# A two-block transformer on one core: the third weight's parts kept in the query tiles, the first norm's sum taken sooner, the last norm scaled in wider pieces

## The chip, the cores and the metric

The kernel runs on one core of one Trainium2 chip. The metric is the device time of one execution in microseconds (us), the median of several runs. All shapes are fixed: 512 tokens of width 1024, all data in fp32.

## What is computed

Two blocks, one after the other. The first mixes tokens with four kinds of heads and adds a gated feed-forward part; the second is a short convolution, a feed-forward part, latent attention, a feed-forward part and a last norm. Cut to what the change touches:

```python
def first_block(x, ...):
    mixed = token_mix(rms_norm(x, norm1_g), w_in, ...)   # one product with w_in, then four kinds of heads
    x = x + mixed @ w_out
    return x + conv_glu_ffn(rms_norm(x, norm2_g), ...)

def second_block(x, ...):
    ...                                                  # short convolution, FFN, latent attention
    h = h + swiglu_ffn(rms_norm_2(h, mla_ffn_norm_g), w13, w2)
    return rms_norm_2(h, final_norm_g)                   # the last norm

def rms_norm(x, g):
    return x * rsqrt(mean(x * x, axis=-1) + EPS) * g
```

## The kernel before, in words

Everything lies transposed: 128 features on the partitions, 512 tokens along a row, so that x is 8 tiles of 128x512. A product of fp32 precision is made from two parts of each operand, a rounded one (h) and what is left (l): three matmuls (h by h, h by l, l by h) for each of 8 steps, 24 for one output tile. `split` (L111) makes a weight's parts: ScalarE copies h (L113), VectorE subtracts (L118). A weight comes by one DMA into one of 3 `raw` buffers, and its parts go into one of 2 `wh` and 2 `wl` buffers, which come free when the product that used them ends.

A norm is put off: the matmuls take x times its gain, and the row factor r (1/rms) is multiplied in when VectorE takes the product out of PSUM. r comes from the sum of squares `acc` (`squares`, L157, each square on ScalarE, each add on VectorE), a matmul with a tile of ones (`mean`, L1543), and Ln, Exp and one Newton step (`rsqrt_wide`, L137).

The first phase, `mix`, is planned by hand. `conduct` (L768) writes TensorE's queue in order: it keeps a count `clk` of TensorE time, steps the products of `w_in` (in the order `ORDER`: sm0, gq0, gk0, then by availability gv0, lq0, lf0, lv0), and between the steps puts the pieces of three lanes of strands, each due at a time that the strand itself gives (`yield`). The first lane holds `mean`, `small` (gates from tile sm0), `gdn0`, `gdn1`; the second the linear attention (`hg0`, `gla`, `hg1`); the third `fox0`, `fox1`. The orders on the other engines come from the tile framework: a priority by place in the program, and readiness by its own cost model; each engine then runs its list in order.

Around the change: `start` (L1511) loads x and the first two weights in pieces and makes their parts; `conduct` steps the two products together (48 matmuls, L782 to L786), then starts the third and the fourth, whose PSUM has tag `fps`; `mean` is due `Y_MEAN` after its strand starts, which is at the end of the first two. Until `mean` is done nothing can be taken out of PSUM; then sm0 is scaled by r (`scaled`, L915), which gives back the first `mm` buffer of PSUM, then gq0 (`convolved`, L949, into a tile z of which there is one in this phase, and a convolution of three VectorE operations, L237). `first_low` (L152 to L154) makes the next weight's subtraction on VectorE stand behind the last operation of r. `small` transposes sm0, makes the gate logarithms on ScalarE, and `Y_SM` later multiplies them (`gg`, L980) with a triangle on TensorE. `hg_bounds` (L1245) are a dozen small operations on ScalarE and VectorE in turn.

`final` (L332) is the last product with the last norm: the last of 8 tiles is made in two halves of 256 tokens, and `write` (L365) multiplies each half's 8 tiles with r, 6 on VectorE and 2 on GpSimd, into `raw` tiles, and stores them two tiles at a time, all from SyncE's queue.

Of the kernel before, what the change touches and what calls it, by code (L numbers as in the profile page):

```python
# [9 lines left out]
F32 = mybir.dt.float32  # L10
F32R = mybir.dt.float32r
# [3 lines left out]
ACTF = mybir.ActivationFunctionType  # L15
ALU = mybir.AluOpType
AX = mybir.AxisListType

S = 512
D = 1024  # L20
KD = D // 128
# [3 lines left out]
CHUNK = 8  # L25


class Builder:
# [108 lines left out]
    def rsqrt_wide(self, ps, scale, tag, n=S, short=False):  # L137


        nc = self.nc  # L140
        r = self.t(tag="u", bufs=3)[:, :n]
        nc.scalar.activation(out=r, in_=ps, func=ACTF.Ln, scale=scale, bias=self.epsD)
        v = self.t(tag="s", bufs=3)[:, :n]
        nc.scalar.activation(out=r, in_=r, func=ACTF.Exp, scale=-0.5)
        if n < S or short:
            nc.vector.tensor_scalar(out=v, in0=ps, scalar1=scale, scalar2=EPS, op0=ALU.mult, op1=ALU.add)
        else:
            nc.scalar.activation(out=v, in_=ps, func=ACTF.Identity, scale=scale, bias=self.epsD)
        nc.vector.tensor_tensor(out=v, in0=v, in1=r, op=ALU.mult)
        nc.vector.scalar_tensor_tensor(out=v, in0=v, scalar=-0.5, in1=r, op0=ALU.mult, op1=ALU.mult)  # L150
        out = self.t(tag=tag, bufs=3 if tag == "u" else 1) if tag else v
        i = nc.vector.scalar_tensor_tensor(out=out, in0=v, scalar=1.5, in1=r, op0=ALU.add, op1=ALU.mult)  # L152
        if short:
            self.first_low = i.ins  # L154
        return out

    def squares(self, xs, adder):  # L157
# [174 lines left out]
    def final(self, w, xs, gi, out):  # L332


        nc = self.nc
        last = KD - 1
        g = [self.gains[:, gi * KD + k : gi * KD + k + 1] for k in range(KD)]
        acc = self.b("acc")
        for c in range(last):
            ps = self.dense(w, c, xs)  # L340
            nc.vector.tensor_tensor(out=self.x[c], in0=self.x[c], in1=ps, op=ALU.add)
            sq = acc if c == 0 else self.t(tag="sq")
            nc.scalar.activation(out=sq, in_=self.x[c], func=ACTF.Square)
            if c:
                nc.gpsimd.tensor_tensor(out=acc, in0=acc, in1=sq, op=ALU.add)
            nc.scalar.activation(out=self.x[c], in_=self.x[c], func=ACTF.Copy, scale=g[c])
        ws = self.weight(w, last, len(xs))
        n = S // 2
        for half in range(2):
            ts = slice(half * n, half * n + n)  # L350
            ps = self.product(ws, xs, ts)
            x = self.x[last][:, ts]
            nc.vector.tensor_tensor(out=x, in0=x, in1=ps, op=ALU.add)
            sq = self.t(tag="sq")[:, :n]
            nc.scalar.activation(out=sq, in_=x, func=ACTF.Square)
            nc.scalar.activation(out=x, in_=x, func=ACTF.Copy, scale=g[last])
            if half:
                self.write(out, 0, r)
            sp = self.pst()[:, :n]
            nc.tensor.matmul(out=sp, lhsT=self.ones, rhs=acc[:, ts], start=True, stop=False)  # L360
            nc.tensor.matmul(out=sp, lhsT=self.ones, rhs=sq, start=False, stop=True)
            r = self.rsqrt_wide(sp, 1.0 / D, None, n)
        self.write(out, 1, r)

    def write(self, out, half, r):  # L365

        nc = self.nc
        n = S // 2
        ts = slice(half * n, half * n + n)
        for i in range(2):  # L370
            y = self.raw.tile([128, CHUNK * 128], F32, tag="raw", name="raw").rearrange("p (k t) -> p k t", t=n)
            for k in range(4):
                eng = nc.gpsimd if k == 1 else nc.vector
                eng.tensor_tensor(out=y[:, k], in0=self.x[4 * i + k][:, ts], in1=r, op=ALU.mult)
                if k % 2:
                    ks = slice(4 * i + k - 1, 4 * i + k + 1)
                    nc.sync.dma_start(out=out[ks, :, ts].rearrange("k p t -> p k t"), in_=y[:, k - 1 : k + 1])


NH = 8  # L380
# [12 lines left out]
class Mla(Builder):  # L393
# [244 lines left out]
TILES = {  # L638
    n: i
    for i, n in enumerate(  # L640
        "sm0 gq0 gq1 gk0 gk1 gv0 gv1 lq2 lk2 lv2 lv3 lq0 lq1 lf0 lf1 lv0 lv1 rq0 rq1 rk0 rk1 fv0 fv1 "
        "gz0 gz1 lz0 lz1 lz2 lz3".split()
    )
}
T_SMALL, T_GQ = TILES["sm0"], TILES["gq0"]
ORDER = (
    "sm0 gq0 gk0 lf1 gq1* lq2 gv0* lq0* lf0 lk2 lv0 lq1* rq0 lv3 gk1* lv2 "
    "rk1 fv0 gv1 lv1 rk0 gz0* rq1 lz0* fv1 gz1 lz3* lz2 lz1*"
)
# [9 lines left out]


Y_FIN, Y_FOX, Y_GDN, Y_SM = 8.3, 8.64, 4.0, 5.33
Y_MEAN = 12.3
C_MEAN = 4.0
C_SILU = 4.8
Y_ROW = 2.66
DUE = 4.78
# [7 lines left out]
class Mix(Mla):  # L674
# [93 lines left out]
    def conduct(self, jobs, lanes):  # L768
# [8 lines left out]
        last = []  # L777
        self.last = last
        xs = [(k, *x) for k, x in enumerate(self.xs)]
        nxt, dense, held = None, [], []  # L780

        two = [(self.stepped(ws, xs, "mm"), jobs.pop(0)) for ws in self.firsts]  # L782
        for i in (0, 0, 1, 1, *(0, 1) * (KD - 2)):
            ps, k = next(two[i][0])
            if k == KD - 1:
                held.append((ps, *two[i][1][2:]))  # L786
        outs, parked, row = list(range(KD)), [], None
        while True:

            for i, lane in enumerate(lanes):  # L790
                if strands[i] is None and lane and all(n in ready for n in lane[0][0]):
                    need, name, gen, rings = lane.pop(0)
# [4 lines left out]
            while held and "mean" in self.over:  # L797
                ps, name, post = held.pop(0)
                t = post(ps)
                if t is not None:  # L800
                    ready[name] = max(self.clk, ready["mean"] + C_MEAN) + t
            if nxt is None:
                job = next((j for j in jobs if j[1] in self.over), None)
                if job:
                    jobs.remove(job)
                    nxt = job, self.weight(self.a["w_in"], job[0], KD)
                elif not jobs and outs:
                    c = outs.pop(0)
                    nxt = (c, None, None, self.out_post(c)), self.weight(self.a["w_out"], c, KD)
# [100 lines left out]
    def scaled(self, dst, after=None, last=None):  # L910


        def post(ps):
            y = self.b(dst[0], bufs=2 if dst[0] in ("lv", "fv") else 1)
            self.nc.vector.tensor_tensor(out=y, in0=ps, in1=self.r, op=ALU.mult)  # L915
            if last is not None:
                return self.silus(y, dst, last)
            self.inp[dst] = y
            return LV + (after(y) if after else 0.0)

        return post
# [589 lines left out]
    def start(self, gi):  # L1511


        idle = self.psm.tile([128, S], F32, tag="lps", name="lps", bufs=2)
        for _ in range(11):
            self.nc.tensor.matmul(out=idle[:, :128], lhsT=self.ones, rhs=self.ones, start=True, stop=True)
        nc = self.nc
        self.x = [self.rt("x") for _ in range(KD)]
        cts = T_SMALL, TILES[ORDER.split()[1][:3]]
        raw = [self.raw.tile([128, CHUNK * 128], F32, tag="raw", name="raw") for _ in cts]  # L1520
        h = [self.wh.tile([128, CHUNK * 128], F32R, tag="wh", name="wh") for _ in cts]
        l = [self.wl.tile([128, CHUNK * 128], F32R, tag="wl", name="wl") for _ in cts]
        steps = (("w", 0, 0), ("x", 0), ("x", 1), ("w", 1, 0), ("x", 2), ("x", 3), ("w", 0, 1), ("x", 4),
                 ("w", 1, 1), ("x", 5), ("x", 6), ("x", 7))
        half = lambda i: slice(i * 512, i * 512 + 512)
        for what, i, *part in steps:
            if what == "x":
                nc.sync.dma_start(out=self.x[i], in_=self.a["xT"][i])
            else:
                cs = half(part[0])  # L1530
                nc.sync.dma_start(out=raw[i][:, cs], in_=self.a["w_in"][cts[i], :, cs])
        self.xs = []
        for what, i, *part in steps:
            if what == "x":
                self.xs.append(self.gained(self.x[i], self.gain(gi, i), "x"))
            else:
                cs = half(part[0])
                self.split(raw[i][:, cs], h[i][:, cs], l[i][:, cs])
        col = lambda t, k: t[:, k * 128 : (k + 1) * 128]
        self.firsts = [[(col(h[i], k), col(l[i], k)) for k in range(KD)] for i in range(2)]  # L1540
        self.acc = self.squares(self.x, nc.vector)

    def mean(self):  # L1543
# [57 lines left out]
@with_exitstack  # L1601
def kernel(ctx, tc, aps, out):
    b = Mix(ctx, tc, aps)
    with b.phase("mix", 2, s=4, sq=3, z=1):
        b.start(0)
        b.mla_consts()
        b.mix_consts()
        b.mix()
    b.rope_pool = ctx.enter_context(tc.tile_pool(name="rope", bufs=1))
    with b.phase("ffn"):  # L1610
        b.consts()
        b.conv_glu(2)
        b.conv_mixer(3)
        b.swiglu(5, aps["w13_a"], aps["w2_a"], b.rope_tables())
    with b.phase("mla", 4, "pt"):
        b.mla(4, 6)
    with b.phase("ffn2"):
        b.swiglu(None, aps["w13_b"], aps["w2_b"], out=(7, out))


# [108 lines left out]
```

## Time and profile before

| | |
|---|---|
| median of 3 runs | 1879.36 us (1879.07 to 1899.09) |
| the profiled execution's own time | 1877.87 us |
| its span | 1876.1 us |
| mean granted clock of TensorE | 0.99 |
| TensorE busy | 97% of the span |
| VectorE busy | 56% |
| ScalarE busy | 39% |
| GpSimd busy | 10% |
| chain that ended last | TensorE 87%, VectorE 6%, ScalarE 4% |

Times in the trace are us from the span's start. A row of the timeline gives an instruction's start, its duration, engine, line, operation, what it writes and reads, and in brackets how long its engine had stood idle and what released it. The ends of matmuls are modelled, so the distance from one start to the next tells more than a duration. The granted clock is 1.00 at 2.4 GHz and 0.50 at 1.2 GHz.

### The profile page before, as it was taken

Reading aid. Unit: us, or ns where it says so; the run is one execution under the profiler, and the core shown is the slowest. Engines: PE = TensorE matmul, PEld = TensorE weight load, DVE = VectorE, ACT = ScalarE, POOL = GpSimd, SP = SyncE. Lnnn points to the kernel's source line nnn. Section 1 sums busy time; section 2 is a strip of 40 time slices with the busy share of each in tenths; the row PEclk is TensorE's granted clock in tenths of the full one; section 3 lists DMA queues with packets and bytes.
Section 4 is the critical chain, followed back from the end, with each engine's and each line's share of the span. In section 5 each row is a group of like instructions: output and inputs, shape, how many; then the busy total and the mean of one; then the engine's idle time right before and its main releaser. Section 6 shows DMA issues by size and latency. Waiting matters only on the chain.

```text
span 1876.1 us, 22127 instructions
## 1 busy us (share of the span) xinstructions
PE 1824.9 (97%) x8631; PEld 1509.4 (80%) x8631; DVE 1055.9 (56%) x1624; ACT 740.0 (39%) x1138; POOL 194.2 (10%) x230
## 2 busy tenths in 40 slices
PE   7899989899999999999999999999999999999997
PEld 5788778778888888888888888888777888888886
DVE  5885886767777733455464444333876454444323
ACT  4644455345444432322343232322667432332322
POOL 2320311220000001111110000000011200000001
PEclk8999999999999999999999999999999999999999
DMA  4111111132222333322222222333222222222332
GB/s 165 46 46 46 57 34 35 62 100 99 101 92 100 98 93 93 99 99 92 101 96 101 96 95 101 93 93 97 80 61 74 78 91 100 92 101 92 99 93 76
DMA packets 53368, 162.62 MB, mean 87 GB/s; under 512 B 6544, under 2 KB 13200, under 8 KB 53264
## 3 DMA queue, kind: packets, MB, share of 16 engines
q1 hardware_dynamic: 53136, 161.21, 26.0%
q8 instruction: 67, 1.10, 0.2%
q14 instruction: 37, 0.30, 0.1%
q10 hardware_dynamic: 128, 0.01, 0.0%
HBM read 157.78 MB, written 2.10 MB: 85 GB/s over the span
## 4 chain that ended last, share of the span: by engine, by line
PE 87%; DVE 6%; ACT 4%; issue 1%; POOL 1%; DMA 0%; SPq 0%; DVEq 0%; ACTq 0%; POOLq 0%
PE mm L131 24%; PE mm L133 24%; PE mm L132 24%; PE mm L715 9%; PE gps L715 2%; PE lps L715 2%; PE fps L715 1%; ACT wh L113 1%; DVE lat L1382 1%; DVE wl L118 1%; POOL s L1320 0%; PE ps L586 0%; PE ps L174 0%; DVE ptl L118 0%; DVE nm L589 0%
## 5 line engine op out<-in xcount | busy, mean ns | idle before, releaser
L113 ACT ACTIVATE wh<-raw 128x1024 fp32r<-128x1024 f32 (+3 forms) x309 | 308.7, 1001 | 763.0 <-PE mm L132 463.5
L131 PE MATMUL mm<-xh,wh 128*128 128x512 f32 x1336 | 522.5, 391 | 0.2 <-ACT xh L182 0.2
L132 PE MATMUL mm<-xl,wh 128*128 128x512 f32 x1336 | 521.3, 390 | 0.5 <-DVE xl L183 0.5
L133 PE MATMUL mm<-xh,wl 128*128 128x512 f32 x1336 | 520.6, 390 | 0.0
L118 DVE TENSOR_TENSOR wl<-raw,wh 128x1024 fp32r<-128x1024 f32 (+4 forms) x301 | 366.2, 1217 | 231.2 <-ACT wh L113 228.3
L132 PEld LDWEIGHTS mm<-xl,wh 128*128 128x128 f32 x1336 | 251.0, 188 | 53.8 <-issue 1.2
L131 PEld LDWEIGHTS mm<-xh,wh 128*128 128x128 f32 x1336 | 251.0, 188 | 53.4 <-issue 1.0
L133 PEld LDWEIGHTS mm<-xh,wl 128*128 128x128 f32 x1336 | 251.0, 188 | 52.1 <-issue 0.2
L131 PE MATMUL mm<-hidh,wh 128*128 128x512 f32 (+1 forms) x614 | 237.0, 386 | 0.0
L133 PE MATMUL mm<-hidh,wl 128*128 128x512 f32 (+1 forms) x614 | 235.5, 384 | 0.0
L132 PE MATMUL mm<-hidl,wh 128*128 128x512 f32 (+1 forms) x614 | 234.1, 381 | 0.0
L715 PE MATMUL mm<-xh,wh 128*128 128x512 f32 x292 | 130.7, 448 | 11.6 <-DVE sm L915 5.6
L133 PEld LDWEIGHTS mm<-hidh,wl 128*128 128x128 f32 x614 | 115.5, 188 | 24.3
L132 PEld LDWEIGHTS mm<-hidl,wh 128*128 128x128 f32 x614 | 115.5, 188 | 23.3
L131 PEld LDWEIGHTS mm<-hidh,wh 128*128 128x128 f32 x614 | 115.8, 189 | 21.7 <-ACT wh L113 0.2
L715 PE MATMUL mm<-xl,wh 128*128 128x512 f32 x292 | 118.0, 404 | 0.9 <-DVE xl L183 0.5
L715 PE MATMUL mm<-xh,wl 128*128 128x512 f32 x292 | 117.9, 404 | 0.2 <-DVE wl L118 0.2
L287 DVE TENSOR_TENSOR u<-mm,rb 128x512 f32<-128x512 f32 x44 | 30.4, 691 | 141.2 <-PE mm L133 141.2
L167 POOL TENSOR_TENSOR z<-z,sq 128x512 f32<-128x512 f32 x31 | 51.8, 1672 | 556.7 <-ACT sq L165 519.0
L283 DVE TENSOR_TENSOR u<-mm,rb 128x512 f32<-128x512 f32 x44 | 30.4, 692 | 90.9 <-PE mm L133 90.8
L715 PEld LDWEIGHTS mm<-xh,wh 128*128 128x128 f32 x292 | 57.4, 197 | 25.0 <-issue 8.5
L113 ACT ACTIVATE hidh<-s 128x512 fp32r<-128x512 f32 x66 | 41.7, 632 | 88.3 <-DVE s L264 57.2
(436 smaller groups left out, 2089.6 us busy)
## 6 DMA issues: line engine op xcount, KB each, us to landing
raw<-in_w_a_dram SPq DMA_DIRECT2D x52, 512.0 KB, 3.3
raw<-in_w_b_dram SPq DMA_DIRECT2D x52, 512.0 KB, 3.2
raw<-in_w_up_dram SPq DMA_DIRECT2D x44, 512.0 KB, 3.2
raw<-in_w_in_dram SPq DMA_DIRECT2D x27, 512.0 KB, 3.2
raw<-in_conv_w_in_dram SPq DMA_DIRECT2D x24, 512.0 KB, 3.2
raw<-in_w_down_dram SPq DMA_DIRECT2D x16, 448.0 KB, 3.3
raw<-in_w_a_dram SPq DMA_DIRECT2D x16, 448.0 KB, 3.3
raw<-in_w_b_dram SPq DMA_DIRECT2D x16, 448.0 KB, 3.2
```

The lines of the kernel that those rows point to most:

```text
L113: nc.scalar.activation(out=h, in_=src, func=ACTF.Copy)
L118: (eng or nc.vector).tensor_tensor(out=l, in0=src, in1=h.bitcast(F32), op=ALU.subtract)
L131: nc.tensor.matmul(out=ps, lhsT=h, rhs=xh, start=(k == 0), stop=False)
L132: nc.tensor.matmul(out=ps, lhsT=h, rhs=xl, start=False, stop=False)
L133: nc.tensor.matmul(out=ps, lhsT=l, rhs=xh, start=False, stop=(k == kt - 1))
L167: eng.tensor_tensor(out=acc, in0=acc, in1=sq, op=ALU.add)
L283: nc.vector.tensor_tensor(out=g, in0=ps, in1=r, op=ALU.mult)
L287: nc.vector.tensor_tensor(out=g, in0=ps, in1=r, op=ALU.mult)
L715: self.nc.tensor.matmul(out=out, lhsT=lhsT, rhs=rhs, start=start, stop=stop)
L1382: nc.vector.copy_predicated(out=at.rearrange("p c (n j) -> p c n j", j=2 * b)[:, :, :, b:], mask=self.lmask[:, lv - 1].rearrange("p (n j) ...
```

## The change

Three things. The third weight (gk0) is loaded in `start` and its parts go into the two tiles `lbd0` and `lbd1`, which the linear attention uses for its query tiles later, so that it needs no `wh` and `wl` buffer; its DMA stands in SyncE's queue behind the last tile of x and ahead of the constants. `Y_MEAN` goes from 12.3 to 2.6 and `C_MEAN`, the planner's count from the sum to the first tile, from 4.0 to 3.6; `first_low` is now the scaling of sm0, so the next weight's subtraction stands behind that. In `final` the tiles times gain go to a tile of their own, `xg`; `write` multiplies four tiles with one VectorE operation in place (at the end two and two), none on GpSimd, with fewer stores, the last two from ScalarE's queue. In the last phase there is one z buffer, not two.

```diff
@@ rsqrt_wide
-        i = nc.vector.scalar_tensor_tensor(out=out, in0=v, scalar=1.5, in1=r, op0=ALU.add, op1=ALU.mult)
-        if short:
-            self.first_low = i.ins
+        nc.vector.scalar_tensor_tensor(out=out, in0=v, scalar=1.5, in1=r, op0=ALU.add, op1=ALU.mult)
@@ final
+        self.scaled_x = self.b("xg", shape=(128, KD * S)).rearrange("p (k t) -> p k t", t=S)
-            nc.scalar.activation(out=self.x[c], in_=self.x[c], func=ACTF.Copy, scale=g[c])
+            nc.scalar.activation(out=self.scaled_x[:, c], in_=self.x[c], func=ACTF.Copy, scale=g[c])
-            nc.scalar.activation(out=x, in_=x, func=ACTF.Copy, scale=g[last])
+            nc.scalar.activation(out=self.scaled_x[:, last, ts], in_=x, func=ACTF.Copy, scale=g[last])
@@ write
-        for i in range(2):
-            y = self.raw.tile([128, CHUNK * 128], F32, tag="raw", name="raw").rearrange("p (k t) -> p k t", t=n)
-            for k in range(4):
-                eng = nc.gpsimd if k == 1 else nc.vector
-                eng.tensor_tensor(out=y[:, k], in0=self.x[4 * i + k][:, ts], in1=r, op=ALU.mult)
-                if k % 2:
-                    ks = slice(4 * i + k - 1, 4 * i + k + 1)
-                    nc.sync.dma_start(out=out[ks, :, ts].rearrange("k p t -> p k t"), in_=y[:, k - 1 : k + 1])
+        k0 = 0
+        for many in (4, 4) if half == 0 else (4, 2, 2):
+            ks = slice(k0, k0 + many)
+            y = self.scaled_x[:, ks, ts]
+            nc.vector.tensor_tensor(
+                out=y, in0=y, in1=r[:, :n].unsqueeze(1).to_broadcast([128, many, n]), op=ALU.mult
+            )
+            eng = nc.scalar if half and k0 == 4 else nc.sync
+            eng.dma_start(out=out[ks, :, ts].rearrange("k p t -> p k t"), in_=y)
+            k0 += many
@@
-Y_MEAN = 12.3
-C_MEAN = 4.0
+Y_MEAN = 2.6
+C_MEAN = 3.6
@@ conduct
-        nxt, dense, held = None, [], []
+        dense, held = [], []
...
+        nxt = jobs.pop(0), self.third_ws
@@ scaled
-            self.nc.vector.tensor_tensor(out=y, in0=ps, in1=self.r, op=ALU.mult)
+            i = self.nc.vector.tensor_tensor(out=y, in0=ps, in1=self.r, op=ALU.mult)
+            if dst[0] == "sm":
+                self.first_low = i.ins
@@ start
+        r3 = self.raw.tile([128, CHUNK * 128], F32, tag="raw", name="raw")
+        nc.sync.dma_start(out=r3, in_=self.a["w_in"][TILES[ORDER.split()[2][:3]]])
+        h3, l3 = (self.b(f"lbd{i}", F32R, shape=(128, 1024)) for i in range(2))
+        self.split(r3, h3, l3)
+        self.third_ws = [(col(h3, k), col(l3, k)) for k in range(KD)]
         self.acc = self.squares(self.x, nc.vector)
@@ tile_two_blocks_kernel
-    with b.phase("ffn2"):
+    with b.phase("ffn2", z=1):
```

## Rows read from the trace of the kernel before

**Rows 1.** Profile page, part 1: busy us, share of the span, instructions.

```profile
PE 1824.9 (97%) x8631; PEld 1509.4 (80%) x8631; DVE 1055.9 (56%) x1624; ACT 740.0 (39%) x1138; POOL 194.2 (10%) x230
```

**Rows 2.** TensorE's waits, 0 to 450 us: total us, times, longest us.

```profile
PE fps L715 <- ACT fpt L1496: 6.4, 2, 4.0
PE mm L715 <- DVE sm L915: 5.6, 1, 5.6
PE gps L715 <- DVE gg L980: 5.5, 1, 5.5
```

**Rows 3.** Stretches of 5 us: length, TensorE busy, granted clock, DMA share, GB/s.

```profile
20.00:25.00 5.00, 3.48 (x8) 0.66 0.29 92
...
40.00:45.00 5.00, 4.14 (x10) 0.50 0.30 105
...
60.00:65.00 5.00, 4.21 (x16) 0.50 0.00 0
```

**Rows 4.** Timeline of TensorE, 17 to 66 us.

```profile
17.75 0.39 PE L715 MATMUL mm<-xh,wl 128*128 128x512 f32 x1
21.33 0.64 PE L715 MATMUL mm<-xh,wh 128*128 128x512 f32 x1 [3.19 <-ACT wh L113]
...
25.16 0.40 PE L715 MATMUL mm<-xh,wl 128*128 128x512 f32 x1
...
34.26 1.02 PE L715 MATMUL gps<-z,ones 128*128 128x512 f32 x2
40.86 0.77 PE L715 MATMUL mm<-xh,wh 128*128 128x512 f32 x1 [5.58 <-DVE sm L915]
...
45.57 0.39 PE L715 MATMUL mm<-xh,wl 128*128 128x512 f32 x1
...
60.78 0.61 PE L715 MATMUL gps<-gg,mixc 128*128 128x16 f32 x2 [5.48 <-DVE gg L980]
...
65.95 0.40 PE L715 MATMUL mm<-xh,wh 128*128 128x512 f32 x1
```

**Rows 5.** Timeline of ScalarE, 18 to 58 us.

```profile
18.80 0.20 ACT L1250 ACTIVATE lb<-lb 128x2 f32<-128x2 f32 x1 [1.22 <-DVE lb L1249]
...
20.24 1.99 ACT L113 ACTIVATE wh<-raw 128x1024 fp32r<-128x1024 f32 x2
...
57.35 0.61 ACT L270 ACTIVATE gk<-gk 128x512 f32<-128x512 f32 x1
```

**Rows 6.** Timeline of VectorE, 15 to 55 us.

```profile
15.06 3.57 DVE L167 TENSOR_TENSOR z<-z,sq 128x512 f32<-128x512 f32 x4
...
18.73 0.69 DVE L167 TENSOR_TENSOR z<-z,sq 128x512 f32<-128x512 f32 x1
...
38.89 1.22 DVE L118 TENSOR_TENSOR wl<-raw,wh 128x1024 fp32r<-128x1024 f32 x1
40.03 0.68 DVE L915 TENSOR_TENSOR sm<-mm,rb 128x512 f32<-128x512 f32 x1
...
52.38 2.31 DVE L237 SCALAR_TENSOR_TENSOR gv<-z,mixp,gv 128x512 f32<-128x512 f32 x3
```

**Rows 7.** Stretches: length, VectorE busy, granted clock, DMA share, GB/s.

```profile
36.00:62.00 26.00, 19.59 (x32) 0.81 0.17 61
62.00:100.00 38.00, 33.67 (x69) 0.95 0.12 42
```

**Rows 8.** DMA issues on the page: KB each, median us to landing.

```profile
raw<-in_w_in_dram SPq DMA_DIRECT2D x27, 512.0 KB, 3.2
```

**Rows 9.** Timeline of GpSimd, 18 to 36 us.

```profile
35.34 0.10 POOL L243 MEMSET z<- 128x3 f32 x1 [17.25 <-PE gps L715]
```

**Rows 10.** Timeline of VectorE, 1861 to 1877 us.

```profile
1864.30 3.05 DVE L374 TENSOR_TENSOR raw<-x,s 128x256 f32<-128x256 f32 x6
...
1869.16 3.16 DVE L374 TENSOR_TENSOR raw<-x,s 128x256 f32<-128x256 f32 x6
```

**Rows 11.** A stretch of the end, columns as in Rows 7.

```profile
1871.00:1874.50 3.50, 1.32 (x4) 0.50 0.87 294
```

## The prediction

> **What bounds the kernel now.** The profile page comes first: TensorE is busy for 97% of the span [rows 1], so time is won only where TensorE stands idle or runs slowly, or at the very end. The list of TensorE's waits then says where: over the mix phase three single waits and one on the fox attention stand out [rows 2]. The timeline shows that three lie before 61 us, and each is followed by slow matmuls [rows 4]; the windows put those at a granted clock of 0.50, the 1.2 GHz level [rows 3]. The reader should price a wait as idle time plus the slow matmuls behind it.
>
> At full rate a matmul starts every 0.2275 us: from 25.16 to 34.26 there are 40 of them in 9.10 us [rows 4]. By that measure:
>
> - Wait 1, the third weight: the last matmul of the first two products starts at 17.75, the next at 21.33; 3.58 less 0.23 is 3.35 us idle. From 21.33 to 25.16 there are 8 steps, 1.82 us at full rate, in 3.83: 2.01 more. Together 5.36.
> - Wait 2, for PSUM: the sum's matmul is over at 35.28, lq0 starts at 40.86: 5.58. The 11 steps to 45.57 take 4.71 instead of 2.50: 2.21. Together 7.79.
> - Wait 3, for gg: 5.48, and the 5.17 us to 65.95 are nearly all at half clock, some 2.4 lost. Together 7.88.
>
> All three cost 21.0 us [rows 3, 4].
>
> **The change part by part.**
>
> *The third weight.* In the kernel before, gk0's weight needs the buffers of the first two, and ScalarE copies it at 20.24, behind the small operations of `hg_bounds` that wait on VectorE in turn [rows 5]. With its own tiles only its DMA is needed, issued behind the last x. By the median of 3.2 us to landing [rows 8] it is there before the first two products end at about 17.98. Nothing is removed: one copy (half of 1.99 us for two, [rows 5]) and one subtraction (1.22, [rows 6]) move forward. Wait 1 should go: 5.36 us.
>
> What it is moved past: the constants' DMAs stand behind it in SyncE's queue and come between nothing (hidden behind the x tiles) and 3.2 us later [rows 8]; I take 1.3, since DMAs in flight overlap. They feed `hg_bounds`, behind which ScalarE makes gv0's parts: from 20.24 that would be 21.5 to 23.8 with copy and subtraction, and TensorE needs them at about 24.5; at 3.2 it would wait about 1.2 us. GpSimd's queue: clearing `lbd` must now wait for gk0's product, and what stands behind it is late with it, but GpSimd is idle for 17.25 us until 35.34 [rows 9], so nothing.
>
> On VectorE the extra subtraction meets the adds of `acc`: four from 15.06, the fifth over at 19.42 [rows 6]; with 1.22 among them, 20.6. ScalarE and VectorE keep to their lists: the copy at 20.24 found its buffers free at 18 and still stood behind `lb` [rows 5]. The Trainium skill ("TensorE: Matmul & The Clock Gate", Architectural detail) says the same of the two queues, strict order; by it the late `acc` costs what stands ahead of it, and were it not so this term would be nothing.
>
> *The sum sooner.* The planner counts 0.648 for a step of three matmuls; 2.6 is passed after the fifth, so the sum's matmul stands behind 15 matmuls of gk0, at 17.98 + 15 x 0.2275 = 21.4 us. `acc` at 20.6 is in time by 0.8; below I allow up to 2 us of waiting. From the sum to sm0 out of PSUM took 34.26 to 40.71, 6.45 us, of which 1.14 was a weight's subtraction between r and sm0 (38.89 to 40.03, [rows 4, 6]), which `first_low` now puts behind. So sm0 is done at 21.4 + 5.3 = 26.7. Its transposes are placed after five steps of gv0: 17.98 + 39 x 0.2275 + 1.03 = 27.9; lq0, which needs the buffer, at 30 or later. Wait 2 should go: 7.79 us. The moved subtraction (lq0's) has from 26.7 to 30 to run; without that cover it is 1.22.
>
> *What is late next.* Every wait is gone only if VectorE keeps up. In TensorE's work the first transposes of `gdn0` stand just behind the products that end at 55.3, less 5.36 and 7.79: at about 42. They need the silu of gk0, which came 3.3 us after the third convolution (52.38 + 2.31 to 57.96, [rows 5, 6]). VectorE did 19.59 us between 36 and 62 [rows 7], with gv0's subtraction 20.8, of which some 2.5 belong to tiles after that point. From 21 us: with no gap 21 + 18.3 + 3.3 = 42.6; at the packing of 62 to 100 us, 33.67 in 38 or 0.886 [rows 7], 45. So TensorE waits 0.6 to 3 us there, plus slow matmuls (1 to 2.4, as behind waits 1 and 3). The logarithms for gg stand in the same queues, ahead of the silus now because `small` is planned before gv0 is done; they wait between nothing and 1 to 2 us. A check on a longer stretch: VectorE's 53.3 us from 36 to 100 and the 1.22 more make 54.5; at 0.886 that is 61.5, from 21 to 82.5, or 17.5 us sooner than 100. I take 3.8 us given back, bounds 0 and 13.
>
> *The end.* Half 0's six VectorE multiplies take 3.05 us and the r of half 1 stands behind them [rows 10]. Two of 1024 columns, at 1.22 like the subtraction of that size [rows 6], take 2.44: 0.6 sooner. Half 1: 3.16 becomes 1.22 + 2 x 0.69 = 2.60, so the last multiply ends 1.2 sooner. But the stores decide: the last 1 MB flows for 3.5 us at 294 GB/s [rows 11], and it can only begin sooner, by the r (0.6) and hardly by the first, wider multiply. I take 0.7, bounds 0 and 1.2. The second issuing queue gains nothing by itself: the Trainium skill ("DMA: Bandwidth & Descriptors", Issuing engines are not separate DMA queues) says that all run on the same 16 engines; with it the end gains 0.7, and 1.2 if a second queue had its own bandwidth. The DMA share of 0.87 in that window agrees with the rule [rows 11]. The copies into `xg` replace copies of the same size, and one z buffer in the last phase is enough for its one use: nothing.
>
> Sum: 21.0 - 3.8 + 0.7 = 17.9. The profiled execution took 1877.87, so 1860.0; the runs' median is 1.49 higher, so 1861.5.
>
> **The rivals.** (Times are medians.)
>
> *A, forecast*: waits 1 and 2 go, wait 3 shrinks to a few us on VectorE: 1861.5, from 1857 to 1867.
>
> *B, all three go*: VectorE's order happens to suit, and the later waits shrink a little with everything earlier. 21.0 + 0.7: 1857.7. For it: VectorE is busy only 19.59 of 26 us now [rows 7], partly because it waited for TensorE. Against: TensorE's 26 us become 20.
>
> *C, wait 3 comes back whole* in front of gg or the silus, or VectorE packs at only 0.80: 54.5 / 0.80 = 68.1, from 21 to 89, 11 us sooner. 21.0 - 7.9 - 1.2 + 0.7 = 12.6 by the one, 11.7 by the other: 1867. For it: VectorE's list is fixed beforehand, and 19.59 in 26 is a packing of only 0.75 [rows 7], which would give 6.6 and 1872.
>
> *D, slower*: VectorE is the bound from the sum to 100 us. Its 54.5 us would then fill all of the 79 us from 21 to 100 at a packing of 0.69; below that the kernel is slower than before. At 0.65 it takes 83.8, 4.8 us past 100, with 0.7 back at the end: 1883.5. Against: both stretches pack better than 0.69 [rows 7].
>
> *E, the end alone works*: the sum's matmul waits for `acc` as long as gk0 had waited for its weight, TensorE being held in order, and sm0 comes no sooner; 0 to 5 us won: 1876. For it only the 0.8 us of margin; against it that `acc` would have to come at 26 or later.
>
> **How the numbers follow.** A 0.50, B 0.20, C 0.24, D 0.03, E 0.03. About 1% is what a measurement of this kernel can tell from no change; that bound is 1860.6. B lies below it, and of A, whose 1861.5 is just above, two fifths (0.20): faster 0.40. D's slower end passes 1898 only at a packing under 0.56, so slower 0.02; the rest, 0.58, is within 1%. The range 1855 to 1872 leaves out D, E and the far ends of B and C.
>
> **What would show it.** In the changed kernel's trace: no idle time before gk0's first matmul, at about 18, and none of the 0.50 windows before 40 us; the matmul of ones behind 15 matmuls of gk0 at 21 to 22; L915 of sm0 over at about 27; lq0 starting without a wait at about 30; the first transposes of `gdn0` at 42 to 45 instead of behind 60.78, with whatever wait is left on VectorE or on a silu; VectorE busy for over 85% from 21 to 80; the last store's flow starting about 0.7 sooner against the last matmul. Wrong would be: the sum's matmul waiting long on z, a wait of over 4 us on gg or on a silu, or gains before 65 us that are lost again by 400.

## The result, and the profile after

The changed kernel takes 1861.26 us (median of 6 runs, 1859.34 to 1871.39) beside 1879.84 us for the kernel before on the same chip: a ratio of 0.9894, 95% interval 0.9849 to 0.9938. (The ratio, here and below, is one of all the runs; that of the two medians is 0.9901.) Executions of one kernel fall into groups 10 to 20 us apart (the kernel before at 1878 to 1882 and at 1896 to 1900), so I go by marks in the traces of the profiled executions first, and by the medians second. The profiled execution of the changed kernel took 1860.22 us with a span of 1858.4; that of before took 1877.87 with 1876.1. The difference to explain is 17.65 us.

Page part 1 of the changed kernel (busy us, share of the span, instructions), beside [rows 1]:

```profile
PE 1818.7 (98%) x8631; PEld 1503.6 (81%) x8631; DVE 1053.5 (57%) x1617; ACT 738.0 (40%) x1138; POOL 193.7 (10%) x226
```

Busy time hardly moves, as it should: the same work is done, and what went is idle and slow time. TensorE's waits of 0 to 450 us in the changed kernel (total us, times, longest us), beside [rows 2]:

```profile
PE fps L716 <- ACT fpt L1500: 6.5, 2, 4.0
PE gps L723 <- ACT gk L268: 2.7, 1, 2.7
```

The fox attention's wait is the same. Of the waits in the first 61 us, gk0's weight has nothing left of 3.2, sm 0.50 of 5.58 and gg 0.34 of 5.48; a new one of 2.72, on ScalarE's silu of gk0, has come. The timeline of TensorE in the changed kernel, beside [rows 4], shows where they stand:

```profile
18.08 0.39 PE L716 MATMUL mm<-xh,wl 128*128 128x512 f32 x1
18.31 0.39 PE L716 MATMUL mm<-xh,lbd 128*128 128x512 f32 x1
...
21.71 1.02 PE L716 MATMUL gps<-z,ones 128*128 128x512 f32 x2
...
28.71 0.66 PE L723 MATMUL gps<-mlac,sm 128*128 128x128 f32 x4 [0.50 <-DVE sm L917]
...
35.88 0.40 PE L716 MATMUL gps<-gg,mixc 128*128 128x16 f32 x2 [0.34 <-DVE gg L984]
...
43.03 0.39 PE L716 MATMUL mm<-xh,wl 128*128 128x512 f32 x1
46.13 0.66 PE L723 MATMUL gps<-mlac,gk 128*128 128x128 f32 x4 [2.72 <-ACT gk L268]
...
93.37 1.13 PE L716 MATMUL fps<-sq,mixc 128*128 128x512 f32 x2 [0.43 <-ACT sq L1460]
```

gk0 starts right behind the first two products; the sum's matmul, which in before stood at 34.26, behind wait 1 and 48 matmuls, stands at 21.71 behind 15. Windows of TensorE in the changed kernel (us, busy, granted clock, DMA share, GB/s), beside [rows 3], which had 0.66, 0.50 and 0.50:

```profile
20.00:25.00 5.00, 5.00 (x22) 1.00 0.24 92
...
40.00:45.00 5.00, 3.42 (x16) 1.00 0.31 107
45.00:50.00 5.00, 3.87 (x21) 1.00 0.00 0
...
60.00:65.00 5.00, 4.87 (x34) 1.00 0.25 94
```

No stretch at 1.2 GHz is left in these windows, not even behind the 2.72 us.

Four marks that both traces have say when the time was won: the first transposes of gk0, 61.66 in before, 46.13 now (15.5 sooner); the fox lane's first wait on `sq`, 110.18 and 93.37 (16.8); a later wait on `xh`, 371.80 and 355.01 (16.8); from the last matmul on `acc` to the span's end 12.48 and 11.66 (0.8). So in these two executions 16.8 us are won before 94 us and kept to the end, and 0.8 at the end. The second mark in the kernel before:

```profile
110.18 1.13 PE L715 MATMUL fps<-sq,mixc 128*128 128x512 f32 x2 [1.32 <-ACT sq L1456]
```

### The profile page after: what moved, and what is told of

It reads as the page before. It is cut to its first block, busy times and chain, and to the rows that moved or that the text cites. A ratio compares the mean times of both kernels' runs of the same rounds, so it can differ in the third digit from the quotient of the medians.

```text
span 1858.4 us, 22098 instructions
## 1 busy us (share of the span) xinstructions
PE 1818.7 (98%) x8631; PEld 1503.6 (81%) x8631; DVE 1053.5 (57%) x1617; ACT 738.0 (40%) x1138; POOL 193.7 (10%) x226
## 4 chain that ended last, share of the span: by engine, by line
PE 86%; DVE 7%; ACT 4%; issue 1%; POOL 1%; DMA 1%; SPq 0%; DVEq 0%; ACTq 0%; POOLq 0%
PE mm L131 24%; PE mm L133 24%; PE mm L132 24%; PE mm L716 7%; PE gps L716 2%; PE lps L716 2%; PE fps L716 1%; ACT wh L113 1%; DVE wl L118 1%; POOL s L1324 1%; DVE lat L1386 1%; PE ps L587 0%; DVE lbd L1335 0%; PE ps L172 0%; DVE ptl L118 0%
## 5 line engine op out<-in xcount | busy, mean ns | idle before, releaser
L118 DVE TENSOR_TENSOR wl<-raw,wh 128x1024 fp32r<-128x1024 f32 (+3 forms) x300 | 365.2, 1217 | 226.9 <-ACT wh L113 223.4
L131 PEld LDWEIGHTS mm<-xh,wh 128*128 128x128 f32 x1336 | 250.9, 188 | 53.4 <-issue 1.0
L222 DVE TENSOR_TENSOR x<-x,mm 128x512 f32<-128x512 f32 x32 | 22.0, 688 | 84.2 <-PE mm L133 84.2
```

The source lines that it names most:

```text
L118: (eng or nc.vector).tensor_tensor(out=l, in0=src, in1=h.bitcast(F32), op=ALU.subtract)
L131: nc.tensor.matmul(out=ps, lhsT=h, rhs=xh, start=(k == 0), stop=False)
L222: self.nc.vector.tensor_tensor(out=self.x[c], in0=self.x[c], in1=ps, op=ALU.add)
```

## The experiments

All kernels compute the whole reference. The fox lane's first wait on `sq` is called the fox mark below: 110.18 in before, 93.37 in the changed kernel. How far it moves by itself shows in the kernel with the end alone changed, whose first phase is that of before:

```profile
112.63 1.12 PE L718 MATMUL fps<-sq,mixc 128*128 128x512 f32 x2 [1.32 <-ACT sq L1459]
```

It stands 2.45 us later behind the same three waits, 0.7 of it because the first products ended later, and most of the rest because the clock came back later behind the waits (granted 0.70 from 25 to 30 us, where before had 1.00). So a difference of fox marks under some 2.5 us shows nothing by itself.

**The three parts, each alone in the kernel before.** The third weight alone is the change's edits of `start` and `conduct`; the sum alone is this:

```diff
@@ rsqrt_wide
-        i = nc.vector.scalar_tensor_tensor(out=out, in0=v, scalar=1.5, in1=r, op0=ALU.add, op1=ALU.mult)
-        if short:
-            self.first_low = i.ins
+        nc.vector.scalar_tensor_tensor(out=out, in0=v, scalar=1.5, in1=r, op0=ALU.add, op1=ALU.mult)
@@
-Y_MEAN = 12.3
-C_MEAN = 4.0
+Y_MEAN = 2.6
+C_MEAN = 3.6
@@ scaled
-            self.nc.vector.tensor_tensor(out=y, in0=ps, in1=self.r, op=ALU.mult)
+            i = self.nc.vector.tensor_tensor(out=y, in0=ps, in1=self.r, op=ALU.mult)
+            if dst[0] == "sm":
+                self.first_low = i.ins
```

and the end alone is the change's edits of `final`, `write` and the last phase.

> The kernel before with the third weight's parts in the query tiles and nothing else. Theory (the three waits are separate and add up): gk0 starts at about 18.0 without a wait, the slow matmuls behind it are gone, 5.4 us in all; the sum is still taken behind gv0, so the waits of 5.6 us for sm0 and 5.5 us for gg stay, and everything behind them moves by 5.4: 5.4 us faster than before, about 1874. Rival (the gain is given back at the next wait): the wait for sm0 grows from 5.6 to about 10 us, because r is not done sooner, and the time stays within 1 us of before.

> The kernel before with the sum's place, its planned cost and the order of the next weight's subtraction changed, but with the third weight as it was, and the end as it was. Theory (waits add up): the 3.2 us before gk0 and the slow matmuls behind it stay (5.4 us), the waits for sm0 and gg go but for 3 to 4 us on VectorE: 16.9 - 5.4 = 11.5 us faster than before, about 1868. Rival (the sooner sum needs the sooner weight, since a sum taken while TensorE was late would have come no later): 5 us or less.

> The kernel before with the end alone changed (four tiles at once, no GpSimd, fewer stores). Theory (the stores' flow decides, and it can begin a little sooner): from the last sum's matmul to the end 11.7 us instead of 12.5, 0.8 us faster. Rival (VectorE's last multiply decides): 1.2 us or more. Rival (the flow decides alone and is not sooner): 0.

TensorE's rows in the third weight alone:

```profile
36.99 0.77 PE L715 MATMUL mm<-xh,wh 128*128 128x512 f32 x1 [6.00 <-DVE sm L916]
57.30 0.61 PE L715 MATMUL gps<-gg,mixc 128*128 128x16 f32 x2 [5.48 <-DVE gg L981]
```

and in the sum alone:

```profile
21.83 0.50 PE L713 MATMUL mm<-xh,wh 128*128 128x512 f32 x1 [3.35 <-ACT wh L113]
...
42.16 0.40 PE L713 MATMUL gps<-gg,mixc 128*128 128x16 f32 x2 [1.42 <-DVE gg L980]
```

with slow matmuls behind the 1.42 (granted clock 0.50 from 44 to 46 us):

```profile
43.41 0.63 PE L713 MATMUL mm<-xh,wh 128*128 128x512 f32 x1
43.83 0.63 PE L713 MATMUL mm<-xl,wh 128*128 128x512 f32 x1
```

The third weight alone takes wait 1 away (the sum's matmul at 29.96, 4.3 sooner, although the first products ended half a us later in that execution), leaves wait 3 as it was and wait 2 at 6.00 instead of 5.58. The fox mark is at 106.67, 3.5 sooner, where 5.4 was expected; the median is 1875.23 (0.9981, 0.9941 to 1.0021). The sum alone leaves wait 1 standing and takes most of the other two: lq0 and sm no longer wait, gg waits 1.42, with some 1.6 us of slow matmuls behind it. The fox mark is at 98.73, 11.45 sooner, where 11.5 was expected; its profiled execution took 1866.35 and the median of ten was 1876.87 (0.9967, 0.9931 to 1.0003). The end alone brings 0.83 from the last matmul on `acc` to the end (11.65), and nothing that its time can show (1879.75 beside 1879.92; 0.9998). All three intervals include 1, so that each part does its share rests on the traces: on the waits, which are there or gone, more than on the marks. By the marks the three add up to 15.8 us beside the 17.65 of all together. The 1.9 left over is less than the fox mark moves by itself, so whether the weight and the sum are worth more at once is open.

**The subtraction at its old place.** The changed kernel with `first_low` as before:

```diff
@@ rsqrt_wide
-        nc.vector.scalar_tensor_tensor(out=out, in0=v, scalar=1.5, in1=r, op0=ALU.add, op1=ALU.mult)
+        i = nc.vector.scalar_tensor_tensor(out=out, in0=v, scalar=1.5, in1=r, op0=ALU.add, op1=ALU.mult)
+        if short:
+            self.first_low = i.ins
@@ scaled
-            i = self.nc.vector.tensor_tensor(out=y, in0=ps, in1=self.r, op=ALU.mult)
-            if dst[0] == "sm":
-                self.first_low = i.ins
+            self.nc.vector.tensor_tensor(out=y, in0=ps, in1=self.r, op=ALU.mult)
```

> The changed kernel with the next weight's subtraction put back between r and sm0's scaling. Theory (from 26 to 44 us VectorE's list is full, so that order inside it moves a wait but not the end of the list): sm0 is 1.2 us later, the transposes of sm0 wait 1.7 us instead of 0.5, the wait for the silu of gk0 shrinks by about as much, and the time stays within 0.5 us of the changed kernel. Rival (each wait is paid for itself): 1.2 us slower than the changed kernel.

Both theories were far off. The profiled execution took 1869.92 us, 9.7 more than the changed kernel's, and the fox mark came at 104.44, 11.1 later; the ten runs go up to 1894.87, with a median of 1876.51 (0.9983, 0.994 to 1.0025). The subtraction itself explains 0.9 of the 11.1 (the wait for sm is 1.44 instead of 0.50), the silu's wait 1.4 more (4.12), and slow matmuls behind that one 1.5 (the same work takes 6.20 us from 47.63 where the changed kernel takes 4.67 from 46.13). The rest stands at 72 us. ScalarE's timeline just ahead of it:

```profile
70.94 0.44 ACT L1325 ACTIVATE s<-s 128x256 f32<-128x256 f32 x1 [0.76 <-POOL s L1324]
71.28 0.58 ACT L1293 ACTIVATE lv<-lps 128x512 f32<-128x512 f32 x1
```

and TensorE's:

```profile
71.91 2.07 PE L718 MATMUL lps<-lq,lk 64*128 64x128 f32 x8 [6.28 <-ACT lv L1293]
```

The copy of lv0 out of PSUM is small, and TensorE had begun to put its input there at 60.71, but in ScalarE's list it stands behind eleven exponentials of the linear attention's levels, which wait for GpSimd one after the other. In the changed kernel it stands behind three of them:

```profile
62.16 0.58 ACT L1293 ACTIVATE lv<-lps 128x512 f32<-128x512 f32 x1
```

The framework makes each list from its own cost model; one subtraction at another place gave another list 40 us later. That was now the theory, and it can be tried by holding the copy alone at its place, with the subtraction still at its old one (the edit above is left out here):

```diff
@@ hg
-        self.nc.scalar.activation(out=vt, in_=self.to_tokens(vt), func=ACTF.Copy)
+        i = self.nc.scalar.activation(out=vt, in_=self.to_tokens(vt), func=ACTF.Copy)
+        self.copied = i.ins if p == 0 else None
...
+            if lv and self.copied is not None:
+                order.enter_context(self.tc.issue_after(self.copied))
```

> The kernel with the next weight's subtraction put back between r and sm0's scaling, whose ScalarE list has lv0's copy behind ten exponentials that wait for GpSimd; here that copy alone is put ahead of all but the first two. Theory (its 6.28 us wait at 72 us, and the slow matmuls behind it, are this place in ScalarE's list and nothing else): the wait falls under 2 us, 7 to 9 us faster than without the pin, about 1862 to 1864. Rival (VectorE, with four multiplies into the query tiles ahead of what TensorE needs next, holds it anyway): the wait moves to the next step and under 3 us are won.

ScalarE's copy in this kernel's timeline:

```profile
61.95 0.60 ACT L1294 ACTIVATE lv<-lps 128x512 f32<-128x512 f32 x1 [0.61 <-PE lps L726]
```

TensorE's 6.28 us wait is gone; what is left there is 0.21 at 61.26, before the transposes that lead to the copy. The fox mark is at 97.10, 7.3 sooner, the profiled execution took 1863.34, 6.6 less, and the median of four is 1863.8 (0.9887, 0.9814 to 0.996). So of the 9.7 us between the profiled executions 6.6 were the place of one copy in ScalarE's list, and some 3 are the subtraction between r and sm0 with what it delays.

**Less work on VectorE.** VectorE is busy for nearly all of the time from 26 to 44 us in the changed kernel (window: length, VectorE busy, granted clock, DMA share, GB/s):

```profile
26.00:44.00 18.00, 17.90 (x35) 1.00 0.32 115
```

If it sets the 2.72 us wait, moving two subtractions (1.22 us each) to GpSimd should shorten it:

```diff
-                    nxt = job, self.weight(self.a["w_in"], job[0], KD)
+                    nxt = job, self.weight(self.a["w_in"], job[0], KD, eng=self.nc.gpsimd if "mean" in self.over and "small" not in self.over else None)
```

> The changed kernel with the subtractions for the weights of lq0 and lf0 on GpSimd, which is idle then, not on VectorE. Theory (the 2.72 us wait for gk0's silu is VectorE's full list): 2.4 us less on VectorE between 27 and 44 us, the third convolution ends at about 41, the wait shrinks to under 1 us, 2 to 2.5 us faster than the changed kernel. Rival (ScalarE holds the silu, with two table loads for lq0's silu that end at 43.6): the wait stays at 2.5 to 3. Rival (GpSimd's subtraction, 2.4 us long, comes late for lf0's product): a new wait of 1 us or more at 30 to 37 us.

It did not: the median of ten is 1866.2 us (0.9931, 0.9887 to 0.9975), the waits for sm, gg and the silu of gk0 are 1.44, 0.71 and 3.41 (0.50, 0.34 and 2.72 in the changed kernel), and the fox mark is at 98.45. VectorE's timeline in that kernel:

```profile
26.07 1.72 DVE L149 TENSOR_TENSOR u<-u 128x512 f32<-128x512 f32 x1
...
34.42 2.38 DVE L983 TENSOR_SCALAR gg<-gg 128x16 f32<-128x16 f32 x1
```

and GpSimd's:

```profile
24.74 2.49 POOL L118 TENSOR_TENSOR wl<-raw,wh 128x1024 fp32r<-128x1024 f32 x1 [1.48 <-ACT wh L113]
...
34.37 2.40 POOL L118 TENSOR_TENSOR wl<-raw,wh 128x1024 fp32r<-128x1024 f32 x1 [0.41 <-ACT wh L113]
```

L983 writes 16 elements of a row; in the changed kernel it takes 0.16 us. Here it takes 2.38 and ends at 36.80, where GpSimd's subtraction ends (36.77). L149, 0.69 in the changed kernel, takes 1.72 and ends 0.56 behind GpSimd's 27.23. So these two operations of VectorE look as if they stood still until GpSimd was done: 1.03 and 2.22 us lost for 2.4 taken off, the first of them inside r, where everything is queued behind it. An operation that read PSUM while GpSimd was at work (L146 at 25.27) took its 0.69 as ever. The Trainium skill ("GPSIMD Engine Reference", Key points) says that the two engines share their way into SBUF, and that VectorE's operations with two SBUF inputs or in a two-port mode contend. L149 has two such inputs, and its row agrees; L983 has one, and whether it ran in a two-port mode no row shows. The experiment says nothing on how much of the 2.72 us is VectorE's.

**What the silu of gk0 waits for.** Marking gk0 in the order list gives its silu a row and table loads of its own, ahead of the others:

```diff
-    "sm0 gq0 gk0 lf1 gq1* lq2 gv0* lq0* lf0 lk2 lv0 lq1* rq0 lv3 gk1* lv2 "
+    "sm0 gq0 gk0* lf1 gq1* lq2 gv0* lq0* lf0 lk2 lv0 lq1* rq0 lv3 gk1* lv2 "
```

> The changed kernel with the silus of gk0 and gq0 in a row of their own, ahead of gv0's convolution (the planner then lets gdn0 start 1.4 us of its count sooner, and ScalarE loads its tables once more each way, 2.6 us). Theory (only gk0's and gq0's silu is needed at 43.4, and both convolutions are done by 39): the wait of 2.72 us goes, about 2.7 us faster than the changed kernel. Rival (ScalarE is the next bound, with 2.6 us more there the gates of lf0 and the copies of the linear attention come later): a new wait of 2 us or more between 55 and 80 us, and no gain.

The wait on the silu is gone, but TensorE stands still for 4.75 us before 50.53, and the lists behind that are others; the median is 1875.07 us (0.9955, 0.9924 to 0.9986). The rival was right that nothing is gained, though its wait came sooner than it said. So I tried it with the lists held. ScalarE in the changed kernel:

```profile
41.71 0.63 ACT L268 ACTIVATE lq<-lq 128x512 f32<-128x512 f32 x1
42.35 1.28 ACT L271 ACT_TABLE_LOAD   x1
43.64 1.28 ACT L268 ACT_TABLE_LOAD   x1
44.93 0.63 ACT L268 ACTIVATE gv<-gv 128x512 f32<-128x512 f32 x1
45.47 0.61 ACT L268 ACTIVATE gk<-gk 128x512 f32<-128x512 f32 x1
```

Between the silus of lq0 and gv0 the exponential's table is loaded and the silu's again, with nothing computed between. One kernel leaves these two loads out, the next also puts gk0's and gq0's silu ahead of gv0's; in both the copy of lv0, one weight copy and one small exponential are held where the changed kernel has them (the lines that hold them are left out here):

```diff
@@ silus
-                ins = self.silu(y, y, i == n - 1)
+                ins = self.silu(y, y, i == n - 1 and name != ("lq", 0))
@@ silus, in the second kernel alone
+        if name == ('gv', 0):
+            self.zs.sort(key=lambda z: ('gk', 'gq', 'gv').index(z[1][0]))
```

> The changed kernel without the two table loads that ScalarE makes between the silu of lq0 (over at 42.34) and that of gv0 (44.93), 1.28 us each; the copy of lv0, one weight copy and one small exponential are held at the places that they have in the changed kernel. Theory 1 (the 2.72 us wait at 46.13 is ScalarE's table loads): gv0's convolution is over at 43.6, its silu starts there instead of at 44.93, gk0's silu and TensorE's transposes follow 1.3 sooner, the wait is 1.4 us, the fox attention's first wait point comes 1.3 sooner than 93.37, time about 1860. Theory 2 (VectorE's chain alone sets it): the wait stays at 2.5 or more, 1861.3. Theory 3 (a small change of the lists costs more than it gives): 1863 or more.

> As e11_no_table_loads_between, and the silus of gk0 and gq0 stand ahead of gv0's in ScalarE's order, so that gdn0's first transposes no longer stand behind gv0's convolution; the exponential eG then stands behind them and has table loads of its own. Theory 1: gk0's convolution is over at 38.9, its silu by about 41, the wait of 2.72 us goes altogether, 2.7 sooner at 93 us, time about 1858.5. Theory 2 (what is put behind, eG, lq0's and gv0's silu, is now late): a wait of 2 us or more in another place between 43 and 60 us, time 1861 or more.

Without the loads, ScalarE's timeline:

```profile
43.16 0.63 ACT L273 ACTIVATE gv<-gv 128x512 f32<-128x512 f32 x1 [1.29 <-DVE gv L240]
```

and TensorE's:

```profile
44.36 0.66 PE L728 MATMUL gps<-mlac,gk 128*128 128x128 f32 x4 [1.41 <-ACT gk L273]
```

The wait falls from 2.72 to 1.41, the fox mark comes 1.8 sooner (91.58; some 0.5 of it from places ahead of these loads; by itself within what the mark moves), and four runs took 1858.21 to 1859.67, median 1859.16 (0.9855, 0.9782 to 0.9928). That is the lowest median of all kernels here; the 2.1 us to the changed kernel, which ran on another occasion, are less than such a comparison can settle. Now the silu of gv0 waits 1.29 us for VectorE's convolution, so half of the 2.72 was ScalarE's loads and the other half is that gk0's silu stands behind gv0's. With gk0's silu ahead, TensorE's first transposes no longer wait, and the wait shows 5 us later:

```profile
49.12 0.38 PE L721 MATMUL gps<-mixb,identb 128*128 128x512 bf16 x1 [1.73 <-issue]
```

The median is 1859.82 us (0.9869, 0.9805 to 0.9933), the fox mark 92.43: no better than without the loads alone. Neither theory came out whole. The direction is the rival's, something put behind is late in its turn, but its wait was to be 2 us or more and the time 1861 or more. What ends the wait the profile does not show. ScalarE's copy `gko<-gps` ends 0.10 us ahead of it, at 49.02, and 0.10 ahead of the 4.75 us wait's end in the kernel above, at 50.43, so a PSUM buffer that comes free late is a likely cause; it was not tried.

**Where the sum stands.** The changed kernel with Y_MEAN 7.8, and with 0.6.

> The changed kernel with the sum due 7.8 behind the first two products, not 2.6: it stands behind 39 matmuls, not 15. Theory (r comes 5.3 us behind the sum, so sm0 is out of PSUM at about 32): lq0 waits some 2.3 us for its buffer, the rest of the plan moves by 2 to 5 us: 1863 to 1867. Rival (only VectorE's full list counts, and the sum's place is free up to there): the time of the changed kernel.

> The changed kernel with Y_MEAN 0.6 in place of 2.6: the sum's matmul stands behind the first step of gk0 (3 matmuls) at about 18.7 us, before the sum of squares is done (21.09 in the changed kernel), so TensorE, which keeps its order, stands still for about 2.4 us. Theory 1 (the chain sum, r, VectorE, ScalarE decides when gdn0's first transposes can start, 46.13 in the changed kernel): this idle time is taken out of the later ones (0.50, 0.34 and 2.72), the sum is 0.6 sooner, the transposes come at 45.5 to 46.5, time 1860 to 1862. Theory 2 (waits add): the 2.4 us come on top, with slow matmuls behind them at times, 1863 to 1866.

With 7.8, lq0 waits for its PSUM buffer again, and TensorE longer for the silu of gk0:

```profile
33.66 0.47 PE L716 MATMUL mm<-xh,wh 128*128 128x512 f32 x1 [2.91 <-DVE sm L917]
...
51.00 1.11 PE L723 MATMUL gps<-mlac,gk 128*128 128x128 f32 x4 [3.79 <-ACT gk L268]
```

The median is 1870.47 us (0.9939, 0.9902 to 0.9976): the mechanism as expected, the price above its range, with a window at 0.50 behind the 3.79. With 0.6 the sum's matmul waits 1.59 us for the sum of squares at 20.80, so that bound is real, and gk0's transposes come at 46.72 behind 2.10, hardly later than the changed kernel's 46.13. But a new wait of 2.04 follows at 73.03, and the time is no measure of the edit: the profiled execution took 1873.82, ten runs 1867.53 to 1889.01 (0.9978, 0.9937 to 1.002). Inconclusive in its time; its trace is used again below.

## Why the prediction was right, and where it was not

The median came out 0.24 us from the forecast, and by the likeliest case, A. That closeness is partly luck: the six executions span 12 us, and some of the steps below were wrong and made up for one another. Step by step:

- *Wait 1 goes.* Right: gk0 starts at 18.31 without a wait. The third weight alone shows it by itself, though by the fox mark it brought 3.5 of the 5.36 us there.
- *The constants are late by 1.3, and gv0's parts with them.* Right in its effect, wrong in its mechanism. The DMA of `mixp` was issued at 14.76 instead of 13.00, but ScalarE read the tile at 17.63, so it had landed by then. What held the operations of `hg_bounds` was VectorE's list: in before the first of them (L1249, at 18.62) stood ahead of the last add of `acc` (18.73, [rows 6]), now it stands behind all of them:

```profile
18.39 2.70 DVE L165 TENSOR_TENSOR z<-z,sq 128x512 f32<-128x512 f32 x3
...
21.07 0.14 DVE L1253 TENSOR_TENSOR lb<-mixp 128x2 f32<-128x2 f32 x1
```

So ScalarE's weight copies began at 22.39, 2.15 later than in before. gv0's parts were ready at 24.69 and TensorE took them without a wait.
- *`acc` in time by 0.8.* It was over at 21.09, not 20.6, with the subtraction among the adds at 1.49 us instead of 1.22; the sum's matmul came at 21.71 behind 15 matmuls. The margin was 0.6; the kernel with the sum at once, which waits 1.59 us for `acc`, shows that the bound is real.
- *sm0 done at 26.7.* Wrong by 2.0: it was done at 28.66. The step that failed is the carrying over of the 6.45 us from sum to sm0. VectorE's subtraction between r and sm0 did go, but in ScalarE's list two weight copies now stand ahead of r's logarithm:

```profile
22.39 2.00 ACT L113 ACTIVATE wh<-raw 128x1024 fp32r<-128x1024 f32 x2
24.29 0.66 ACT L142 ACTIVATE u<-gps,epsD 128x512 f32<-128x512 f32 x1
```

and on VectorE:

```profile
27.97 0.69 DVE L917 TENSOR_TENSOR sm<-mm,rb 128x512 f32<-128x512 f32 x1
```

In before the logarithm started as the sum's matmul ended (35.28):

```profile
35.32 0.69 ACT L142 ACTIVATE u<-gps,epsD 128x512 f32<-128x512 f32 x1
```

Of TensorE's time this cost the 0.50 us wait of sm's transposes, which could have started at 28.2. VectorE's list is full behind r, so part of the 2.72 us at 46.13 may come from it too; that is argued and was not tried.
- *Wait 2 goes.* Right: lq0 starts at 31.29 without a wait.
- *Wait 3 shrinks to 0.6 to 3 us on VectorE or on a silu.* Right in place and size (0.34 on gg and 2.72 on the silu of gk0). The first transposes themselves came at 46.13, where 42 to 45 was said. The prediction let VectorE's work begin at 21; but the stretch that it was read from begins at 36, 1.7 us behind the start of the sum's matmul (34.26), while 21 is 0.4 ahead of where the prediction put that matmul (21.4). VectorE's first operation on the sum, 36.04 in before, came at 24.99. From there the 18.3 us with no gap give 43.3, and gv0's convolution ended at 43.61. The 3.3 us to the silu, on the other hand, came out at 2.5. They hold a table load that the prediction does not name (in before at 55.52), and without the two loads the silu is done 1.2 us behind the convolution. So the 2.72 us are not all VectorE's: half of them are ScalarE's two table loads. VectorE was nearly as full as forecast, 84% of 21 to 80 us where over 85% was said. Windows of VectorE in the changed kernel (columns as in [rows 7]):

```profile
21.00:80.00 59.00, 49.44 (x107) 1.00 0.18 64
36.00:62.00 26.00, 20.31 (x47) 1.00 0.24 81
```

Beside [rows 7], 19.59 of 26 became 20.31. VectorE did not become the bound up to 100 us, so rival D was far off. Rival C took 0.75 as a packing that VectorE's list might have; with 17.90 of 18 us from 26 to 44 it packed far better.
- *Slow matmuls of 1 to 2.4 us behind what is left.* Wrong, to the good: the clock stayed at 1.00. No trace here shows that it had to: in the sum alone it fell to 0.50 behind a wait of only 1.42 us. Given back were 0.50, 0.34 and 2.72, 3.6 in all, for the 3.8 that was taken. That more idle time and no slow matmuls made up for one another is luck. 21.0 less 3.6 is 17.4, less 0.33 by which the first products ended later in this execution is 17.1, and 16.8 were measured. The other 0.3 I have not traced, and it is less than the mark moves by itself.
- *The end, 0.7.* Measured 0.82. Half 0 took 2.36 (2.44 forecast) beside 3.05, half 1 2.43 (2.60) beside 3.16 [rows 10]:

```profile
1847.42 2.36 DVE L373 TENSOR_TENSOR xg<-xg,s 128x1024 f32<-128x1024 f32 x2
...
1851.60 2.43 DVE L373 TENSOR_TENSOR xg<-xg,s 128x1024 f32<-128x1024 f32 x3
```

- *`first_low` as a matter of 1.14 us.* The weakest step, though nothing in the result shows it. Undone, it costs 9.7 us between the profiled executions, most of it in a list 40 us later. The prediction priced every moved instruction at its place and took the rest of the lists as given, but the lists are made anew for every edit. That the new ones were no worse was luck that the sum does not contain: with the other list the profiled execution took 1869.92, near the upper end of the range, and the median of ten, 1876.51, lies above it, by a mechanism that none of the rivals names.

## What to carry to other kernels

Where one engine is near full, price a stall as idle time plus the slow matmuls behind it, take it out where the chain starts, and expect to get back all but what the next engine in the chain can't keep up with. When a stretch of one engine's work is carried over to a new start, carry it from the same event, not from the window's edge. Before believing a small edit's price where a framework orders the engines' lists, compare the lists: a copy that slid behind instructions waiting for another engine cost more here than the edit itself. And before putting work on GpSimd to relieve VectorE while VectorE's chain is the one waited for, look whether VectorE's operations get longer beside it; here that cost more than it took off.

## What the runs showed of the hardware that was not expected

The length of an idle stretch alone did not say at what rate TensorE went on. Behind 2.72 us (changed kernel, 46.13) the clock stayed at 1.00; behind 3.19 (before, wait 1) and 3.98 it fell to 0.50, and behind only 1.42 (the sum alone, 42.16), after 17 us of work without a break, it fell to 0.50 as well. How long it stays there differs too. The same 3.98 us wait for `fpt` stands in both these traces; in the kernel with the sum at once TensorE then worked without a break at the lower rate for some 20 us (windows of TensorE, columns as above):

```profile
260.00:265.00 5.00, 4.40 (x13) 0.50 0.01 3
...
275.00:280.00 5.00, 5.00 (x23) 0.50 0.00 0
280.00:285.00 5.00, 5.00 (x21) 0.61 0.27 101
```

while in the changed kernel it was back at 1.00 within the window that begins 7 us behind the wait:

```profile
255.00:260.00 5.00, 2.13 (x6) 0.68 0.32 107
260.00:265.00 5.00, 5.00 (x21) 0.64 0.00 0
265.00:270.00 5.00, 5.00 (x37) 1.00 0.00 0
```

The waits for `xh` that follow, at 355.01 in the changed kernel and 367.74 in the other, were 12.7 us apart where the fox marks were 2.7 apart, so this and a second, shorter stretch cost 10 us with the work unchanged. What decides how long it lasts no run here shows. That an operation of VectorE took as long as a whole operation of GpSimd beside it (2.38 us for one of 0.16) was the other surprise.
